# Hybrid decoder block: the output projection as seven block products, with the block sums made on GpSimd and the second token half finished tile by tile

## The chip, the cores and the metric

The kernel runs on one core of one Trainium2 chip. The metric is device time per execution in microseconds. The kernel before takes 1583.07 us, the median of three runs (1582.68 to 1584.89).

## The reference

One decoder block on 1024 tokens of width 1024, in float32. The step that changes is the one between the two branches and the FFN:

```python
merged = jax.nn.sigmoid(gate_a) * branch_a + jax.nn.sigmoid(gate_b) * branch_b
x = x + merged @ w_out[l]

h2 = rms_norm(x, ln2_g[l])
x = x + (jax.nn.silu(h2 @ w_ffn_gate[l]) * (h2 @ w_ffn_up[l])) @ w_ffn_down[l]
```

`branch_a` is the retention branch times `w_ret_out`, `branch_b` the attention branch times `w_attn_out`. `w_out` is 1024 x 1024.

## The kernel before, in words

Every float32 matrix product is made of three passes. Each operand is split into a high half (a rounded copy, type float32r, made by ScalarE) and a low half (the operand less the high half, made by VectorE); the passes are high x high, high x low and low x high, added up in PSUM. A helper `halves` or `split` is one such pair of instructions.

Most of the large products (the value projection, the gates, the FFN) already run in a form with seven block products in place of eight (the Strassen-Winograd form): each operand is cut into 2 x 2 blocks, sums of blocks are made first, and seven products P1 to P7 are added up in PSUM in such an order that each output block comes from one or two banks. The output projection does not; it runs as a plain product.

The order of the stages around the change:

- Branch A (`ba{n}`, lines 1103 to 1114). For each of 8 row blocks n of 128 features, `dense` loads a 512 KB slab of `w_ret_out`, splits it and makes 48 matmuls, 24 for each half of 512 tokens. `evac` then reads the gate `ta` and the other branch's part `mb` from DRAM, makes the merged row block `ms` on VectorE (two instructions) and splits it into the tiles M[0] and M[1] (tag B of the pool `act`). These hold the merged matrix transposed: features on the partitions, tokens along the row.
- Output projection (lines 1247 to 1304). x is loaded into x2. For each half `nh` of 512 output columns, the four slabs of `w_out` are loaded and split ahead; then for each of the 8 token tiles t, 24 matmuls (8 feature blocks x 3 passes) fill one PSUM bank of the tag `acc` (three banks in turn), and VectorE adds half of it to x2 (line 1283; the factor of a half belongs to the gates).
- In the second half of columns a token tile is complete, and its work up to the FFN's operands follows: ScalarE squares the row with an accumulator (line 1288), GpSimd makes the reciprocal root (two small instructions, lines 97 and 99), ScalarE scales the row (line 1293), TensorE transposes it in eight 128 x 128 pieces, and VectorE multiplies by the norm's gain (`columns`, lines 1207 to 1234). For the first four tiles each 512 columns are also split into a high and a low half there; for the last four, VectorE makes three block sums. `s2_part` and `a22_part` split one token tile of two of those sums. `early_t` makes sums of FFN weights, `prep_to` splits FFN weights, `release` makes low halves that were held back.

What sets the order: each engine runs its instructions one after the other. A planner orders them by priority and by its own costs; `high_priority(offset=AHEAD)` moves the loads and splits of weights ahead. Inside `in_order(engines)` the instructions of these engines keep the order in which they are written. For VectorE and ScalarE such a block (`late`) begins at the last token tile, for TensorE (`first`) at the FFN's first product. All DMAs here are issued from SyncE (SP), one after the other; an issue that must wait holds those behind it. A tile of a pool that takes over the memory of earlier ones waits for all their readers; x2 takes the memory of the tiles of branch A's `evac`. In PSUM, an instruction that writes a bank waits for the one that still has to read it. There are eight banks: three of tag `acc`, one of `pv`, two of `s`, two of `t`.

The functions that the change touches:

## Time and profile before

| | us |
|---|---|
| median of the runs | 1583.07 |
| span of the profiled execution | 1583.3 |
| TensorE busy | 1570.7 (99%) |
| VectorE busy | 990.2 (63%) |
| ScalarE busy | 720.7 (46%) |
| GpSimd busy | 354.9 (22%) |

The profiled execution has a span of 1583.3 us from its first to its last instruction, 0.2 us from the median, so a sum made on the trace holds for the runs as it is. Branch A runs from 766 to 853 us of the span, the output projection from 853 to 946. In a row of the profile the engines are PE (TensorE's matmuls), PEld (its weight loads), DVE (VectorE), ACT (ScalarE), POOL (GpSimd) and SP (SyncE, the DMA issues); `wo<-wotw,m` says that a tile wo is written from the tiles wotw and m; L1283 is a line of the kernel. A time in square brackets is how long the engine sat idle before the instruction, and behind the arrow stands what ended the wait.

### The profile page before, as it was taken

The numbers are of one execution on the slowest core, as the hardware profiler recorded it, in microseconds if no ns is written. First come the engines' busy times: TensorE is split into PE (matmuls) and PEld (weight loads), VectorE is DVE, ScalarE is ACT, GpSimd is POOL, SyncE is SP. The second block draws the span as 40 slices with busy tenths as digits, with TensorE's granted clock in tenths as the row PEclk, the third lists the DMA queues.
The fourth block names the chain that finished last, engine by engine and source line by source line (L and its number), as shares of the span: only waits on it lengthen the run. The fifth ranks groups of instructions, "written<-read, shape, count | busy, mean of one in ns | idle before, by whom it ended". The sixth has DMA issues, their size and how long they took to land.

```text
span 1583.3 us, 20873 instructions
## 1 busy us (share of the span) xinstructions
PE 1570.7 (99%) x7483; PEld 1307.1 (83%) x7483; DVE 990.2 (63%) x1776; ACT 720.7 (46%) x1446; POOL 354.9 (22%) x303
## 2 busy tenths in 40 slices
PE   9999999999999999999999999999999999999998
PEld 8887888888888888888888888888888888888886
DVE  6469978777657663878544369444444444678656
ACT  5258877844233333544221256333333333344445
POOL 2000000000055441000000013555555555100001
PEclk9999999999999999999999999999999999999999
DMA  6564655440364455654545102333333333762333
GB/s 204 157 176 124 205 193 150 143 140 34 126 225 150 134 166 184 229 189 156 177 149 199 54 0 74 106 104 106 112 105 100 101 110 109 285 250 84 98 103 124
DMA packets 148886, 223.13 MB, mean 141 GB/s; under 512 B 9195, under 2 KB 81709, under 8 KB 147246
## 3 DMA queue, kind: packets, MB, share of 16 engines
q1 hardware_dynamic: 148780, 221.79, 43.3%
q8 instruction: 59, 0.97, 0.3%
q14 instruction: 45, 0.37, 0.1%
q10 hardware_dynamic: 2, 0.00, 0.0%
HBM read 149.67 MB, written 67.37 MB: 137 GB/s over the span
## 4 chain that ended last, share of the span: by engine, by line
PE 90%; ACT 6%; DVE 3%; issue 1%; POOL 0%; POOLq 0%; ACTq 0%; DVEq 0%
PE fA L1337 15%; PE fB L1337 8%; PE dA L1618 7%; PE wA L841 7%; PE dxP L1618 6%; PE fC L1337 4%; PE wB L841 3%; PE va L686 3%; ACT sc L466 2%; PE acc_g L157 2%; PE vP L686 2%; PE acc_g L158 2%; PE acc_g L159 2%; PE wo L1277 2%; PE wo L1276 2%; PE acc_ba L159 2%
## 5 line engine op out<-in xcount | busy, mean ns | idle before, releaser
L1618 PE MATMUL dA<-dwP,daP 128*128 128x512 f32 x528 | 120.6, 389 | 0.0
L1618 PEld LDWEIGHTS dA<-dwP,daP 128*128 128x128 f32 x528 | 99.0, 188 | 20.7 <-DVE dwP L133 0.2
L1618 PE MATMUL dxP<-dwP,daP 128*128 128x512 f32 x396 | 90.2, 389 | 0.0
L1618 PEld LDWEIGHTS dxP<-dwP,daP 128*128 128x128 f32 x396 | 74.3, 188 | 15.4
L157 PE MATMUL acc_g<-h,wh_g 128*128 128x512 f32 x192 | 75.5, 393 | 0.1
L158 PE MATMUL acc_g<-h,wh_g 128*128 128x512 f32 x192 | 75.2, 392 | 0.0
L159 PE MATMUL acc_g<-h,wl_g 128*128 128x512 f32 x192 | 75.1, 393 | 0.0
L466 ACT ACTIVATE sc<-sc,nm 128x257 f32<-128x257 f32 (+1 forms) x128 | 62.5, 492 | 27.1 <-DVE nm L463 26.7
L451 POOL COPY sc<-nsink 128x4 f32<-128x4 f32 x32 | 13.1, 412 | 274.4 <-PE pT L484 157.1
L1406 POOL TENSOR_TENSOR xf<-xf 128x512 f32<-128x512 f32 x40 | 61.2, 1531 | 30.4 <-issue 28.9
L1348 POOL TENSOR_TENSOR xf<-xf 128x512 f32<-128x512 f32 x33 | 49.4, 1496 | 54.3 <-ACT t_1P L130 22.4
L463 DVE CUSTOM_DVE_ANT_0 sc<-s,amask,nsink 128x256 f32<-128x256 f32 (+1 forms) x128 | 54.1, 461 | 9.8 <-PE s L460 9.5
L1358 ACT COPY xf<-fA 128x512 f32<-128x512 f32 x44 | 25.7, 586 | 74.4 <-PE fA L1337 74.4
L133 DVE TENSOR_TENSOR dwP<-wd,dwP 128x512 fp32r<-128x512 f32 x77 | 52.8, 685 | 6.0 <-ACT dwP L130 6.0
L130 ACT CAST dwP<-wd 128x512 fp32r<-128x512 f32 x77 | 47.4, 616 | 9.4 <-PE dA L1618 7.1
L157 PE MATMUL acc_bb<-ay,wh_bb 128*128 128x512 f32 x128 | 51.2, 400 | 0.0
L1523 POOL TENSOR_TENSOR rs_f<-tot,mhalf 128x1 f32<-128x1 f32 x8 | 4.8, 606 | 205.4 <-DVE tot L1520 205.4
L158 PE MATMUL acc_bb<-ay,wh_bb 128*128 128x512 f32 x128 | 50.3, 393 | 0.0
L159 PE MATMUL aq<-h,wl_aq 128*128 128x512 f32 x128 | 50.2, 392 | 0.0
L157 PE MATMUL aq<-h,wh_aq 128*128 128x512 f32 x128 | 50.1, 392 | 0.0
L158 PE MATMUL aq<-h,wh_aq 128*128 128x512 f32 x128 | 50.1, 391 | 0.0
L159 PE MATMUL acc_bb<-ay,wl_bb 128*128 128x512 f32 x128 | 50.1, 391 | 0.0
(794 smaller groups left out, 4356.9 us busy)
## 6 DMA issues: line engine op xcount, KB each, us to landing
act_d<-xf SPq DMA_DIRECT2D x77, 256.0 KB, 2.1
daP<-act_d SPq DMA_DIRECT2D x21, 512.0 KB
q_d<-stg SPq DMA_DIRECT2D x8, 1024.0 KB
q<-q_d SPq DMA_DIRECT2D x32, 256.0 KB, 6.5
ay_d<-q SPq DMA_DIRECT2D x8, 1024.0 KB
ay<-ay_d SPq DMA_DIRECT2D x4, 2048.0 KB, 14.2
wr_daP<-act_d SPq DMA_DIRECT2D x14, 512.0 KB, 3.7
wr_g<-in_w_in SPq DMA_DIRECT2D x12, 512.0 KB, 5.9
```

The lines of the kernel that those rows point to most:

```text
L133: return nc.vector.tensor_tensor(out=lo, in0=raw, in1=f32(hi), op=ALU.subtract)
L157: nc.tensor.matmul(pt, hi[:, k, :], xh, start=(k == 0), stop=False)
L158: nc.tensor.matmul(pt, hi[:, k, :], xl, start=False, stop=False)
L159: nc.tensor.matmul(pt, lo[:, k, :], xh, start=False, stop=(k == 7))
L463: nc.vector.tensor_tensor_reduce(out=sc[:, j, 0:nk], in0=pt[:, jj * 256:jj * 256 + nk], in1=mk, scale=1.0, scalar=nsink[:, 4 * g + j:4 * g ...
L466: nc.scalar.activation(sc[:, j, 0:nk + 1], sc[:, j, 0:nk + 1], AF.Exp, scale=-1.0, bias=nm[:, j:j + 1], accum_out=den[:, j:j + 1])
L686: nc.tensor.matmul(vbanks[pr][tt], x_[:, c], w[:, u, :], start=(fresh and k + z == 0), stop=(k == 3 and z == 2), skip_group_check=not fresh)
L841: nc.tensor.matmul(pt, o[:, w, k, :], v, start=(first and k + z == 0), stop=(k == 3 and z == 2), skip_group_check=not first)
L1337: nc.tensor.matmul(pt, o[:, w, k, :], v, start=(first and k + z == 0), stop=(k == 3 and z == 2), skip_group_check=not first)
L1348: nc.gpsimd.tensor_tensor(out=dst[q], in0=dst[q], in1=sg[q], op=ALU.mult)
L1406: nc.gpsimd.tensor_tensor(out=o, in0=a, in1=b, op=op)
L1618: nc.tensor.matmul(banks[tt], a[:, u, c], w[:, v, :], start=(fresh and f + z == 0), stop=(f == NP - 1 and z == 2), skip_group_check=not fresh)
```

## The change

The output projection becomes seven block products. The merged matrix is cut into four blocks by feature half (kh) and token half, `w_out` into b11, b12, b21, b22. P1, P2 and P4 take blocks of the merged matrix as they are. P3, P5, P6 and P7 take sums of blocks.

Branch A runs its row blocks in the order 0, 4, 1, 5, 2, 6, 3, 7, so that after each second one the four blocks' rows are there; GpSimd makes four sums of 128 x 512, and each is stored to a DRAM tensor `ms_d`. Only three of the four blocks are split in `evac`. In the projection the sums are loaded back (1 MB each, `load_sum`) into the place of the low half and split there (`sum_halves`). The sums of `w_out` are made on VectorE and GpSimd (`sub2`), the halves of the weights in `wsplit`, two steps of 1024 columns each.

P2, P1, P5 and P6 run whole (`by_k`, 48 matmuls each). Then P3 runs by token tile for the first token half (`by_t`, 12 matmuls for each tile), and P7 and P4 by token tile for the second. P1, P6, P7 and P4 use the same four banks `vbank` one after the other; P2, then P5 and P3, use the banks of the tags `s` and `t`. `gain` adds a bank to one half of the columns of x2. `ln2_a` is the square and the reciprocal root, `ln2_b` the scaling. The blocks `late` and `first` now begin before P2. The block sums of the token tiles 4 and 5 in `columns` move from VectorE to GpSimd. The places of the FFN's operands in M[0] and M[1] (m0, m1) change with the products.

```diff
--- before.py
+++ after.py
@@ -63,6 +63,7 @@
     v_d = dram.tile([P, NB, D], F32, name="v_d")
     rk_d = dram.tile([8, P, S], F32, name="rk_d")
     rg_d = dram.tile([8, P, S], F32, name="rg_d")
+    ms_d = dram.tile([4, 4, P, 512], F32, name="ms_d")
     act_d = dram.tile([7, NF // 2, P, 512], F32, name="act_d")
 
     def ps(tag, bufs, name):
@@ -1090,28 +1091,41 @@
 
 
     M = [None, None]
-
-    def mview(k, t, z):
-        return M[k // 4][:, t, (2 * (k % 4) + z) * P:(2 * (k % 4) + z) * P + P]
-
     wdp = ctx.enter_context(tc.tile_pool(name="wdp", bufs=2, side="right"))
     with tc.tile_pool(name="w3", bufs=1) as w3:
-        for n in range(8):
-            if n % 4 == 0:
-                big(M, "B", n // 4, f"m{n // 4}")
+        for n in range(2):
+            big(M, "B", n, f"m{n}")
+        m0, m1 = (m.rearrange("p (q a) (b c) -> p q (a b) c", q=4, b=2) for m in M)
+        places = {(0, 0): (m0, 0), (1, 0): (m0, 2), (1, 1): (m1, 2)}
+        parts = {}
+        for n in (0, 4, 1, 5, 2, 6, 3, 7):
+            kh, k = n // 4, n % 4
 
             def evac(half, pt):
                 c = slice(half * 512, half * 512 + 512)
                 mb = w3.tile([P, 512], F32, tag="mb", bufs=3, name="mbr")
                 nc.sync.dma_start(mb, mb_d[n, :, c])
-                s = w3.tile([P, 512], F32, tag="ms", bufs=2, name="ms")
                 ta = w3.tile([P, 512], F32, tag="ta", bufs=3, name="tar")
                 nc.sync.dma_start(ta, tb_d[n, :, c])
+                s = w3.tile([P, 512], F32, tag=f"ms{kh}{half}", bufs=2, name=f"ms{kh}{half}")
                 nc.vector.scalar_tensor_tensor(out=s, in0=ta, scalar=1.0, in1=pt, op0=ALU.add, op1=ALU.mult)
                 nc.vector.tensor_tensor(out=s, in0=s, in1=mb, op=ALU.add)
-                s = s.rearrange("p (t s) -> p t s", s=P)
-                halves(s, *(mview(n, slice(4 * half, 4 * half + 4), z) for z in range(2)))
+                if (kh, half) in places:
+                    v, q = places[kh, half]
+                    halves(s, v[:, q, k, :], v[:, q + 1, k, :])
+                parts[kh, half] = s
             dense(w_ret_out, n * P, YG, evac, f"ba{n}")
+            if kh:
+                a11, a21, a12, a22 = (parts.pop(i) for i in ((0, 0), (0, 1), (1, 0), (1, 1)))
+                nc.gpsimd.tensor_tensor(out=a22, in0=a21, in1=a22, op=ALU.add)
+                nc.sync.dma_start(ms_d[0, k], a22)
+                nc.gpsimd.tensor_tensor(out=a21, in0=a11, in1=a21, op=ALU.subtract)
+                nc.sync.dma_start(ms_d[2, k], a21)
+                nc.gpsimd.tensor_tensor(out=a11, in0=a22, in1=a11, op=ALU.subtract)
+                nc.sync.dma_start(ms_d[1, k], a11)
+                nc.gpsimd.tensor_tensor(out=a12, in0=a12, in1=a11, op=ALU.subtract)
+                nc.sync.dma_start(ms_d[3, k], a12)
+
 
 
     w4 = ctx.enter_context(tc.tile_pool(name="w4", bufs=1))
@@ -1227,7 +1241,7 @@
                 nc.vector.tensor_tensor(out=a1[:, 2 * q + 1, :, c], in0=o, in1=f32(hi), op=ALU.subtract)
         if half:
 
-            eng = nc.vector
+            eng = nc.gpsimd if t < 6 else nc.vector
             a11, a12, a21, a22 = (xf[:, q, :, c] for q in range(4))
             eng.tensor_tensor(out=a21, in0=a21, in1=a22, op=ALU.add)
             eng.tensor_tensor(out=a11, in0=a21, in1=a11, op=ALU.subtract)
@@ -1235,80 +1249,203 @@
 
     def s2_part(t):
         c = slice(t % 4 * P, t % 4 * P + P)
-        halves(xf[:, 0, :, c], s12[:, 0, :, c], s12[:, 1, :, c])
+        halves(xf[:, 0, :, c], m0[:, 0, :, c], m0[:, 1, :, c])
 
     def a22_part(t):
         c = slice(t % 4 * P, t % 4 * P + P)
-        halves(xf[:, 3, :, c], s3a[:, 0, :, c], s3a[:, 1, :, c])
-
-
-    s12, s3a = (m.rearrange("p (q a) (b c) -> p q (a b) c", q=4, b=2) for m in M)
-
-    for t in range(NB):
-        nc.sync.dma_start(x2[:, t, :], x[t * P:t * P + P, :])
-    for nh in range(2):
-        nsl = slice(nh * 512, nh * 512 + 512)
...
-        else:
-            a1 = act.tile([P, 4, 4, 512], F32R, tag="A", name="a1")
-            xf = act.tile([P, 4, 4, 512], F32, tag="A", name="xf")
-            load(0)
-            load(1)
-        for t in range(NB):
-            pt = acc(f"wo{nh}{t}")
-            for k in range(8):
-                hi, lo = ws[k // 2]
-                mh, ml = mview(k, t, 0), mview(k, t, 1)
-                nc.tensor.matmul(pt, mh, hi[:, k % 2, :], start=(k == 0), stop=False)
-                nc.tensor.matmul(pt, mh, lo[:, k % 2, :], start=False, stop=False)
-                nc.tensor.matmul(pt, ml, hi[:, k % 2, :], start=False, stop=(k == 7))
-            if nh == 1 and t == NB - 1:
-                late = in_order(nc.vector.engine, nc.scalar.engine)
-                late.__enter__()
-                prep_to(2)
-                prep_to(4, True)
-            nc.vector.scalar_tensor_tensor(out=x2[:, t, nsl], in0=pt, scalar=0.5, in1=x2[:, t, nsl], op0=ALU.mult,
-                                           op1=ALU.add)
-            if nh == 1:
...
+        halves(xf[:, 3, :, c], m1[:, 0, :, c], m1[:, 1, :, c])
+
+
+    def blk(y, z):
+        return w_out[y * 512:y * 512 + 512, z * 512:z * 512 + 512].rearrange("(k p) n -> p k n", p=P)
+
+    def two(v, c):
+        return v[:, 2 * c:2 * c + 2]
+
+    def slots4(tags, name):
+        return [[slot(t_, [2, 512], F32R, f"wo{name}{c}{u}") for u, t_ in enumerate(tags)] for c in range(2)]
+
+    def wsplit(src, dst, eng=None):
+        for c in range(2):
+            nc.scalar.copy(dst[c][0], src[c])
+            (eng or nc.vector).tensor_tensor(out=dst[c][1], in0=src[c], in1=f32(dst[c][0]), op=ALU.subtract)
+
+    def sub2(eng, o, p, q):
+        for c in range(2):
+            eng.tensor_tensor(out=o[c], in0=p[c], in1=q[c], op=ALU.subtract)
+
+    W = {}
+    with tc.high_priority(offset=AHEAD):
+        b11, b21 = raw_pair([2, 512], "b11"), raw_pair([2, 512], "b21")
+        for y, b in ((1, b21), (0, b11)):
+            for c in range(2):
+                nc.sync.dma_start(b[c], two(blk(y, 0), c))
+        W["P2"] = slots4(("tw", "tw"), "P2")
+        wsplit(b21, W["P2"])
+        wdp.tile([P, 56], F32, name="pad_wdp", bufs=1)
+        W["P1"] = slots4(("wh", "wl"), "P1")
+        wsplit(b11, W["P1"])
+
+    wob = act.tile([P, 16, 512], F32, tag="A", name="wob")
+    sA = act.tile([P, 4, 4, 512], F32R, tag="A", name="sA")
+    b12, b22, t2 = ([two(wob[:, 4 * i:4 * i + 4], c) for c in range(2)] for i in range(3))
+    XA = {"P1": (m0, 0), "P2": (m0, 2), "P3": (m0, 0), "P4": (m1, 2), "P5": (sA, 0), "P6": (sA, 2), "P7": (m1, 0)}
+
+    def load_sum(pr, i):
+        v, q = XA[pr]
+        nc.sync.dma_start(f32(v[:, q + 1]), ms_d[i].rearrange("k p t -> p k t"))
+
+    def load_x(half, z):
+        nc.sync.dma_start(x2[:, 4 * half:4 * half + 4, z * 512:z * 512 + 512],
+                          x[half * 512:half * 512 + 512, z * 512:z * 512 + 512].rearrange("(t p) n -> p t n", p=P))
+
+    def sum_halves(pr):
+        v, q = XA[pr]
+        for c in range(2):
+            hi, lo = two(v[:, q], c), two(v[:, q + 1], c)
+            nc.scalar.copy(hi, f32(lo))
+            nc.vector.tensor_tensor(out=lo, in0=f32(lo), in1=f32(hi), op=ALU.subtract)
+
+    wide = [[m0[:, 2 + u, 2 * c:2 * c + 2, :] for u in range(2)] for c in range(2)]
+
+    nc.sync.dma_start(wob[:, 0:4], blk(0, 1))
+    load_sum("P5", 0)
+    load_x(0, 0)
+    nc.sync.dma_start(wob[:, 4:8], blk(1, 1))
+    load_sum("P6", 1)
+    load_sum("P7", 2)
+    load_x(1, 1)
+    load_x(0, 1)
+    load_x(1, 0)
+
+    vbank = [ps("pv", 1, "wo0"), acc("wo1"), acc("wo2"), acc("wo3")]
+    obank = {}
+
+    def obanks(pr):
+        obank[pr] = [ps("s", 2, f"wo{pr}{i}") for i in range(2)] + [ps("t", 2, f"wo{pr}{i}") for i in (2, 3)]
+        return obank[pr]
+
+    def wmm(pr, k, tt, first, last, tracked):
+        v, q = XA[pr]
+        bank = (obank["P5" if pr == "P3" else pr] if pr in ("P2", "P5", "P3") else vbank)[tt]
+        w = W[pr][k // 2]
+        c = slice(tt * P, tt * P + P)
+        for z, (u, y) in enumerate(((0, 0), (0, 1), (1, 0))):
+            nc.tensor.matmul(bank, v[:, q + u, k, c], w[y][:, k % 2, :], start=(first and z == 0), stop=(last and z == 2),
+                             skip_group_check=not tracked)
+
+    def by_k(pr, hooks=()):
+        fresh = pr in ("P2", "P1", "P5")
+        for k in range(4):
+            for tt in range(4):
+                wmm(pr, k, tt, fresh and k == 0, k == 3, fresh)
+            if k in dict(hooks):
+                dict(hooks)[k]()
+
+    def by_t(pr, tt):
+        for k in range(4):
+            wmm(pr, k, tt, False, k == 3, False)
+
+    def gain(half, tt, z, bank):
+        v = x2[:, 4 * half + tt, z * 512:z * 512 + 512]
+        nc.vector.scalar_tensor_tensor(out=v, in0=bank, scalar=0.5, in1=v, op0=ALU.mult, op1=ALU.add)
+
+    lnr = {}
+
+    def ln2_a(t):
+        m2 = tiny.tile([P, 1], F32, tag="m2", name="m2")
+        hxs[t] = wo.tile([P, D], F32, tag="hx", bufs=2, name="hx")
+        nc.scalar.activation(hxs[t], x2[:, t, :], AF.Square, scale=1.0 / 32.0, accum_out=m2)
+        lnr[t] = rstd_of(m2, 1, f"ln2_{t}")
+
+    def ln2_b(t):
+        nc.scalar.activation(hxs[t], x2[:, t, :], AF.Copy, scale=lnr[t])
+
+    late = in_order(nc.vector.engine, nc.scalar.engine)
+    late.__enter__()
+    first = in_order(nc.tensor.engine)
+    first.__enter__()
+
+    obanks("P2")
+    sub2(nc.vector, b11, b12, b11)
+    sum_halves("P5")
+    sum_halves("P7")
+    by_k("P2")
+
+    for tt in range(4):
+        gain(0, tt, 0, obank["P2"][tt])
+    W["P5"] = slots4(("tw", "tw"), "P5")
+    wsplit(b11, W["P5"])
+    sub2(nc.gpsimd, t2, b22, b11)
+    load(0)
+    sub2(nc.gpsimd, b21, b21, t2)
+    sub2(nc.gpsimd, b12, b22, b12)
+    by_k("P1")
+
+    for tt in range(4):
+        gain(0, tt, 0, vbank[tt])
+    load_sum("P3", 3)
+    W["P6"] = wide
+    wsplit(t2, W["P6"])
+    sum_halves("P6")
+    obanks("P5")
+    by_k("P5")
+
+    for tt in range(4):
+        gain(1, tt, 1, obank["P5"][tt])
+    W["P3"] = slots4(("wh", "wl"), "P3")
+    wsplit(b22, W["P3"])
+    sum_halves("P3")
+    W["P7"] = slots4(("tw", "tw"), "P7")
+    wsplit(b12, W["P7"])
+    by_k("P6")
+
+    W["P4"] = wide
+    wsplit(b21, W["P4"], nc.gpsimd)
+    load(1)
+    a1 = act.tile([P, 4, 4, 512], F32R, tag="A", name="a1")
+    xf = act.tile([P, 4, 4, 512], F32, tag="A", name="xf")
+    for tt in range(4):
+        gain(0, tt, 1, vbank[tt])
+    for tt in range(4):
+        by_t("P3", tt)
+        gain(0, tt, 1, obank["P5"][tt])
+        ln2_a(tt)
+        if tt > 1:
+            columns(tt - 2)
+        ln2_b(tt)
+    early_t(0, 2)
+    for tt in range(4):
+        t = 4 + tt
+        by_t("P7", tt)
+        gain(1, tt, 1, vbank[tt])
+        if tt == 0:
+            columns(2)
+        by_t("P4", tt)
+        if tt == 3:
+            prep_to(2)
+            prep_to(4, True)
+        gain(1, tt, 0, vbank[tt])
+        ln2_a(t)
+        if tt == 3:
+            release()
+        columns(t - 1)
+        ln2_b(t)
+        if tt == 0:
+            early_t(1, 2)
+        if tt > 1:
+            s2_part(t - 2)
+        if 0 < tt < 3:
+            a22_part(t - 1)
+    s2_part(6)
+    prep_to(5)
 
     s4 = [slot("tw", [2, 512], F32R, f"s4{z}") for z in range(4)]
     prep_to(6)
 
     X = {}
-    for pr, (t_, q) in {"P1": (a1, 0), "P2": (a1, 2), "P6": (s12, 0), "P5": (s12, 2), "P7": (s3a, 2),
-                        "P4": (s3a, 0)}.items():
+    for pr, (t_, q) in {"P1": (a1, 0), "P2": (a1, 2), "P6": (m0, 0), "P5": (m1, 2), "P7": (m0, 2),
+                        "P4": (m1, 0)}.items():
         X[pr] = [(t_[:, q, k, :], t_[:, q + 1, k, :]) for k in range(4)]
     X["P3"] = [(s4[k // 2][:, k % 2, :], s4[2 + k // 2][:, k % 2, :]) for k in range(4)]
 
@@ -1436,8 +1573,6 @@
     LA = 4
     f1 = None
     early = []
-    first = in_order(nc.tensor.engine)
-    first.__enter__()
     for i, (j, pr) in enumerate(seq):
         if i == 16:
             first.__exit__(None, None, None)
@@ -1460,13 +1595,13 @@
                 for z in range(2):
                     k = slice(2 * z, 2 * z + 2)
                     halves(src[:, k], hi[:, k], lo[:, k])
-            pieces(xf[:, 2], s12[:, 2], s12[:, 3])
+            pieces(xf[:, 2], m1[:, 2], m1[:, 3])
             prep_to(8)
 
             for z in range(2):
                 k = slice(2 * z, 2 * z + 2)
                 nc.vector.tensor_tensor(out=xf[:, 0, k], in0=xf[:, 3, k], in1=xf[:, 0, k], op=ALU.subtract)
-            pieces(xf[:, 0], s3a[:, 2], s3a[:, 3])
+            pieces(xf[:, 0], m0[:, 2], m0[:, 3])
             prep_to(10)
             early_t(0, 4)
             a22_part(NB - 2)
```

33 lines of the change are left out of this document (removed).

## The prediction

> **What bounds the kernel now.** I read the page first, for the engine that sets the time.
>
> ```profile
> span 1583.3 us, 20873 instructions
> ...
> PE 1570.7 (99%) x7483; PEld 1307.1 (83%) x7483; DVE 990.2 (63%) x1776; ACT 720.7 (46%) x1446; POOL 354.9 (22%) x303
> ...
> PEclk9999999999999999999999999999999999999999
> ...
> PE 90%; ACT 6%; DVE 3%; issue 1%; POOL 0%; POOLq 0%; ACTq 0%; DVEq 0%
> ```
>
> TensorE (PE) is busy 99% of the span at full granted clock and carries 90% of the chain of waits. A matmul removed is time gained, as long as PE is never made to wait; a wait put on PE is time lost one for one. Next the busy time by stretches: branch A (766 to 853 us), the first and second column half of the output projection (853 to 897, 903 to 946).
>
> ```profile
> 766.00:853.00 87.00, 87.00 (x387) 72.06 (x386) 44.41 (x59) 20.27 (x27) 0.00 (x0) 1.00 0.55 173
> 853.00:897.00 44.00, 44.00 (x196) 36.44 (x195) 10.84 (x14) 4.91 (x6) 0.00 (x0) 1.00 0.30 110
> 897.00:903.00 6.00, 6.00 (x28) 4.99 (x27) 3.96 (x6) 0.99 (x1) 0.00 (x0) 1.00 0.94 316
> 903.00:946.00 43.00, 43.00 (x218) 36.08 (x217) 25.76 (x40) 23.57 (x36) 7.88 (x14) 1.00 0.01 3
> ```
>
> The columns are the stretch's length, busy us (and instructions) of PE, weight load, DVE, ACT and POOL, then clock, DMA share and GB/s. PE is busy for the whole of every row: no wait is left in this stage. POOL (GpSimd) does nothing until 897. The instructions of the two stages, first and last start:
>
> ```profile
> L157 PE MATMUL acc_ba<-yg,wh_ba x128: 389/389/478, 766.1 to 852.5; 128*128 128x512 f32 x128
> ...
> L1275 PE MATMUL wo<-wotw,m x64: 389/389/477, 853.2 to 943.6; 128*128 128x512 f32 x64
> ...
> L1277 PE MATMUL wo<-wowh,m x64: 389/389/393, 855.0 to 945.4; 128*128 128x512 f32 x64
> ```
>
> A matmul lasts 389 ns, but they are pipelined: branch A's 384 take 87.0 us, 0.2267 us each. That pitch, not 389 ns, is what one is worth. The chain of waits around the end of the stage:
>
> ```profile
> 945.79 0.87 PE h2T L1215 x8
> 946.66 5.46 PE fA L1337 x24
> 952.12 0.87 PE h2T L1215 x8
> 953.00 5.46 PE fC L1337 x24
> ```
>
> Eight transposes of one token tile cost PE 0.87 us, and the last tile's VectorE work is covered by 24 matmuls of the FFN, 5.46 us. The change keeps both.
>
> **The change part by part.** *Matmuls.* Before: 2 column halves x 8 tiles x 24 = 384. After: 7 products x 48 = 336. 48 fewer x 0.2267 = **-10.9 us**. The eight sets of transposes stay.
>
> *Sums in branch A.* 16 POOL additions and 16 stores of 256 KB. The nearest rows:
>
> ```profile
> L1406 POOL TENSOR_TENSOR xf<-xf 128x512 f32<-128x512 f32 x40 | 61.2, 1531 | 30.4 <-issue 28.9
> ...
> act_d<-xf SPq DMA_DIRECT2D x77, 256.0 KB, 2.1
> ```
>
> 4 x 1.53 = 6.1 us on POOL in every 21.8 us (two row blocks), on an engine that is idle there; DVE and ACT lose the splitting of one quarter of the blocks. Cost: nothing, hidden behind branch A's matmuls at 55% DMA share. Only the last four are exposed. On SP's queue there are 14 issues more (16 stores, 4 loads of sums, 4 fewer of x, 2 fewer of w_out), half a microsecond each by the row below, in a queue that has less than one issue per us to make.
>
> ```profile
> 856.59 4.20 SPq L1248 DMA_DIRECT2D x<-in_x  x8
> ```
>
> *Loads of the first products.* The last block sum of branch A is known at 854.8. What follows it now:
>
> ```profile
> 854.13 0.69 DVE L1111 TENSOR_TENSOR ms<-ms,mbr 128x512 f32<-128x512 f32 x1
> ...
> 861.80 0.69 DVE L1283 SCALAR_TENSOR_TENSOR x<-wo,x 128x512 f32<-128x512 f32 x1 [5.24 <-DMA x<-in_x]
> ```
>
> ```profile
> GB/s 0 0 0 0 0 0 0 0 0 0 0 82 174 282 206 364 419 406 406 419 419 419 419 419 419 419 419 419 419 419 387 210 0 0 0 0 0 0 0 0
> ```
>
> (slices of 0.63 us from 850 to 875 us). Four POOL additions end at 856.4, 857.9, 859.4, 861; each store lands 2.1 us later. Then P5's sum (1 MB) is issued at 858.6, P7's at 860, P6's at 861.6, and the first quarter of x at 863, since x2 takes the memory that the last sums leave. At some 0.41 MB per us, 2.5 us per MB, and about 2 us before the first bytes, they land at 863, 865.6, 868 and 870.6. DVE and ACT are in written order here: split P5's sum, split P7's sum, four gains of P2 (which need that x), then split P5's weights. The prices of a split of 1024 and of ordinary 512 steps:
>
> ```profile
> 843.86 1.22 DVE L133 TENSOR_TENSOR wowl<-wrx_wo,wowh 128x1024 fp32r<-128x1024 f32 x1
> ...
> 895.34 1.06 ACT L130 CAST wotw<-wr_wo 128x1024 fp32r<-128x1024 f32 x1
> ...
> 901.44 0.69 DVE L1183 TENSOR_TENSOR wr_f<-wrx_f,wr_f 128x512 f32<-128x512 f32 x1 [2.00 <-DMA wrx_f<-in_w_ffn_gate]
> ...
> 938.58 0.69 DVE L559 TENSOR_TENSOR m<-xf,m 128x512 fp32r<-128x512 f32 x1 [0.83 <-ACT m L558]
> ```
>
> Gains 870.6 to 873.2, first half of P5's weights 874.4. PE reaches P5 after P2 and P1, at 853.1 + 2 x 10.9 = 874.9. I take **0**, but the cover is half a microsecond. If SP instead issues in written order, with the load of b12 behind the four stores (861) and 6.3 MB ahead of P7's sum, that sum lands at 878.5, and P5 starts near 885.8: **+10.9**. These are the ends; I stay at the lower, since b12 and b22 are ready from 850.5. The other weight work (POOL's t2, b21, b12, the splits of P6, P3, P7) ends 5 us or more before its product.
>
> *Second half, tile by tile.* This decides. One token tile's work in the kernel now, DVE, ACT and POOL of the same tile:
>
> ```profile
> 907.81 0.69 DVE L1283 SCALAR_TENSOR_TENSOR x<-wo,x 128x512 f32<-128x512 f32 x1 [1.98 <-PE wo L1277]
> 908.42 1.28 DVE L1223 TENSOR_TENSOR xf<-h2T,bcol 128x512 f32<-128x512 f32 x2
> 910.23 0.69 DVE L1227 TENSOR_TENSOR a<-xf,a 128x512 fp32r<-128x512 f32 x1 [0.53 <-ACT a L1226]
> 912.39 0.69 DVE L1227 TENSOR_TENSOR a<-xf,a 128x512 fp32r<-128x512 f32 x1 [1.46 <-ACT a L1226]
> ```
>
> ```profile
> 908.54 1.06 ACT L1288 ACTIVATE hx<-x 128x1024 f32<-128x1024 f32 x1 [1.09 <-DVE x L1283]
> 909.51 0.18 ACT L1288 ACTIVATION_READ_ACCUMULATOR hx<-x 128x1 f32 x1
> 909.60 0.60 ACT L1226 CAST a<-xf 128x512 fp32r<-128x512 f32 x1
> 910.69 1.15 ACT L1293 ACTIVATE hx<-x,rs_ln 128x1024 f32<-128x1024 f32 x1 [0.49 <-POOL rs_ln L99]
> ```
>
> ```profile
> 909.78 0.22 POOL L97 TENSOR_SCALAR ve_ln<-m 128x1 f32<-128x1 f32 x1 [3.51 <-ACT hx L1288]
> 910.08 0.58 POOL L99 TENSOR_TENSOR rs_ln<-ve_ln,mhalf 128x1 f32<-128x1 f32 x1
> ```
>
> From gain to last low half DVE needs 5.3 us (907.8 to 913.1), with waits for ACT inside. Today PE brings a tile every 6.3 us (5.44 + 0.87) and nothing on PE waits for a gain: the next tile goes to another bank. After the change P7 and P4 of a tile follow each other on the same bank, and DVE must read P7's result between them (gain on column half 1), else P4 would be added to it. So PE waits for that gain, and the gain stands in DVE's written order behind everything of the tile before: its last gain, two multiplies and low halves, t-sums, the P3-sum splits, each behind ACT. I follow them with 0.65 us per DVE step (1.28 for two), 0.60 per ACT cast, 1.24 for the square with its accumulator, 0.95 for POOL's two, 1.12 for the scaling, and 0.25 from DVE's end to the next matmul. Time 0 is the end of the tile's P4 on PE, which would be ready for the next P4 at 0.87 + 12 x 0.2267 = 3.6.
>
> - P4 of tile 6: gain 0.7, square 2.0, POOL 3.0, scaling 4.1, ACT half of the a22 piece 4.7, DVE half 5.4, gain 6.05, P4 at 6.3: wait 2.7.
> - P4 of tile 7: one more split pair ahead of it (s2 piece of tile 4): 3.4.
> - P4 of tile 5: gain 0.7, square 2.0, cast, low, multiply, cast, low 5.3, two weight sums 6.6, gain 7.3, P4 at 7.5: 3.9, and DVE comes 0.9 late from the tile before: 4.8.
> - P4 of tile 4: from tile 0's transposes (907.1) DVE has 12 steps, 7.8 us, and waits 6.2 for ACT, where tile 1's scaling, tile 2's square and tile 3's square stand between the casts; with 0.25 P4 starts 14.2 later. PE brings P3 of tile 3, tile 1's transposes, P7 and tile 2's transposes, 7.2 us: 7.0 (1.2 of it ahead of tile 2's transposes).
> - Tile 0's transposes: its reciprocal root stands on POOL behind the split of P4's weights (two of 1024, 2 x 3.06 from 897.8): 1.4.
>
> Sum **+19.3 us**. The lower end of the waits: DVE free whenever P7 ends, then each P4 waits for the gain alone, 0.69 + 0.25, in four tiles 3.8 us.
>
> The longest wait of PE for another engine in this trace is short, so nothing here shows PE after a longer one:
>
> ```profile
> PE warm L266 <- DVE wk L240: 1.0, 1, 1.0
> ```
>
> The Trainium skill, page "TensorE: Matmul & The Clock Gate", Part 1, says that PE's clock falls to half after an idle window of about 3.4 us and comes back after a busy one; by that two or three of my waits would be followed by a slow patch, and no run here shows it.
>
> *Sum.* -10.9 + 0 + 0 + 19.3 = +8.4 us on the profiled execution: 1583.3 + 8.4 = 1591.7. That execution's span lies 0.2 us above the median, 1583.07, so I forecast **1591.5 us**.
>
> **The rivals.**
>
> (a) *DVE keeps up.* If the tile chain fits under 3.6 us of PE, each P4 waits only for its own gain: -10.9 + 3.8 = -7.1, **1576**. For it: POOL takes the three sums of tiles 4 and 5. Against: the 5.3 us chain above, and the written order on DVE and ACT. It turns faster once all waits together are under 10.9 us.
>
> (b) *Waits near the saving.* Without the backlog at tiles 4 and 5 (7.0 and 4.8 become 3.0 and 3.9), waits of 13 less a few steps of DVE at 0.60: **1580 to 1586**, no change.
>
> (c) *P5's operands late*, by SP's order or by transfers that share the queues, up to +10.9: **1602**. For it: margin 0.5 us. Against: 419 GB/s in the row above, all 16 engines.
>
> (d) *A slow clock after the two longest waits*: 12 matmuls each at twice 0.2267, +2.7 twice: **1597**. For it: nothing in this trace, whose clock is 1.00 in every row; against it: nothing either. It is the page's rule above.
>
> (e) *P7 waits as well.* The a22 pieces write the block that P7 reads, other columns of it. If the planner takes this as a conflict, P7 of tiles 6 and 7 starts behind the piece (5.5 instead of 0.9) and P4 one gain later: 2.9 more in each, **1597**.
>
> **How the numbers follow.** Forecast 0.45, with 1588 to 1595 as its own range; (a) 0.11, (b) 0.12, (c) 0.15, (d) 0.12, (e) 0.05. A measurement of this kernel tells some 0.2%, 3.2 us, from no change. Faster (below 1580): (a) and the edge of (b), 0.13; same 0.12; slower 0.75. The range goes from (a) to (c): 1577 to 1602.
>
> **What would show it.** In the profile after: 336 matmuls of the projection; PE waits for DVE on the bank of the P7 and P4 products, four of them, 2.7 to 6 us; DVE's idle time before the low halves put down to ACT. P5's first matmul within 1 us of P1's last, or (c). A granted clock below 1 after the long waits, or (d). The saving alone, with PE busy in every row between 853 and 936, would prove me wrong; so would waits at P4 near 1 us.

## The result, and the profile after

The changed kernel takes **1607.04 us** (median of 4 runs, 1604.04 to 1609.28) against 1583.98 us (1582.68 to 1584.96, 4 runs) for the kernel before on the same chip: ratio 1.0147, 95% interval 1.0133 to 1.0162. It is 23 us slower, where I had forecast 8.4, and it lies above the end of my range.

The page after, span and engines:

```profile
span 1602.2 us, 20889 instructions
PE 1563.7 (98%) x7435; PEld 1298.7 (81%) x7435; DVE 1020.0 (64%) x1792; ACT 730.7 (46%) x1456; POOL 406.4 (25%) x333
```

48 matmuls are gone (7483 before, 7435 now) and PE's busy time fell by 7.0 us, yet the span grew by 18.9: PE now waits. The view of PE's waits (engine, line and tile; what it waited for; us in total, times, longest):

```profile
PE wo L1334 <- DVE x L1351: 13.9, 4, 4.7
PE woP L1334 <- DVE x L1351: 7.7, 1, 7.7
PE woP L1334 <- DVE woP L1271: 2.1, 1, 2.1
PE h2T L1229 <- DVE xf L1237: 1.9, 2, 1.2
```

None of these rows exists before, where the longest wait of PE for another engine was 1.0. L1351 is `gain`: four waits of P4's matmuls, and one of P5's. PE's timeline through the stage (start, us, instruction; in square brackets the idle time before it):

```profile
880.31 0.76 PE L1334 MATMUL woP<-woP,sA 128*128 128x512 f32 x1 [7.66 <-DVE x L1351]
883.14 12.36 PE L1334 MATMUL woP<-woP,sA 128*128 128x512 f32 x47 [2.07 <-DVE woP L1271]
895.34 11.04 PE L1334 MATMUL wo<-m,sA 128*128 128x512 f32 x48
906.22 8.33 PE L1334 MATMUL woP<-woP,m 128*128 128x512 f32 x36
...
927.66 4.36 PE L1334 MATMUL wo<-m,m 128*128 128x512 f32 x12 [2.65 <-DVE x L1351]
...
939.13 3.02 PE L1334 MATMUL wo<-m,m 128*128 128x512 f32 x12 [3.46 <-DVE x L1351]
...
948.81 3.02 PE L1334 MATMUL wo<-m,m 128*128 128x512 f32 x12 [3.06 <-DVE x L1351]
...
952.46 2.98 PE L1334 MATMUL wo<-woP,m 128*128 128x512 f32 x12
960.17 5.10 PE L1334 MATMUL wo<-m,m 128*128 128x512 f32 x12 [4.73 <-DVE x L1351]
...
965.90 3.00 PE L1474 MATMUL fA<-a,t_0P 128*128 128x512 f32 x12
```

The stage begins with P2 at 850.73 and the FFN's first product starts at 965.90: 115.2 us. Before, PE's timeline has it from 853.21 to 946.42, 93.2 us. So the stage is 22.0 longer, which is -10.9 for the matmuls and **+32.9** of losses. (In this execution branch A begins 2.5 us earlier than before, ahead of any edited line; that is no gain of the change, and the runs of before differ among themselves by 2.3. Where times of the two are compared below, they are counted from the start of P2.) The losses fall into two places:

- **P5**, 12.0 us. P1 ends at 872.49; P5 would take 10.88, and P6 starts at 895.34.
- **The tile loops**, 21.0 us. From 906.22 to 965.90 are 59.7 us, for 144 matmuls (32.6) and seven sets of transposes (6.1).

In both, some of the loss is no wait: 12 matmuls of P4 last 4.36 and 5.10 where others last 3.02, and P5's 47 last 12.36 where 10.8 are due (P6's 48 last 11.04). The rows by stretches show it in the granted clock (the third number from the end), then DMA share and GB/s:

```profile
865.00:877.00 12.00, 7.65 (x34) 6.01 (x32) 6.66 (x3) 3.26 (x4) 12.00 (x5) 0.96 1.03 381
877.00:890.00 13.00, 7.62 (x25) 5.87 (x26) 13.00 (x16) 8.31 (x9) 0.35 (x1) 0.65 0.84 295
...
915.00:930.00 15.00, 10.47 (x50) 8.17 (x49) 9.65 (x16) 8.32 (x12) 1.76 (x5) 0.90 0.01 1
...
960.00:975.00 15.00, 14.83 (x64) 12.28 (x65) 10.25 (x17) 7.58 (x17) 0.79 (x2) 0.84 0.00 0
766.00:850.70 84.70, 84.70 (x375) 70.16 (x374) 42.28 (x52) 16.68 (x21) 16.77 (x12) 1.00 0.59 196
```

The last row is branch A: PE is busy all 84.7 us while GpSimd makes 12 sums. That part is hidden, as predicted.

**Why P5 is late.** The timelines of SP's issues, then of DVE, ACT and POOL between branch A and P5:

```profile
861.36 0.32 SPq L1127 DMA_DIRECT2D ms_d<-ms  x1
861.78 0.37 SPq L1296 DMA_DIRECT2D sA<-ms_d  x1
863.64 0.38 SPq L1299 DMA_DIRECT2D x<-in_x  x1
...
864.62 0.53 SPq L1296 DMA_DIRECT2D m<-ms_d  x1
```

```profile
868.65 6.49 DVE L1307 TENSOR_TENSOR sA<-sA 128x1024 fp32r<-128x1024 f32 x2 [11.20 <-ACT sA L1306]
876.82 2.74 DVE L1307 TENSOR_TENSOR m<-m 128x1024 fp32r<-128x1024 f32 x2 [1.69 <-ACT m L1306]
879.49 2.47 DVE L1351 SCALAR_TENSOR_TENSOR x<-woP,x 128x512 f32<-128x512 f32 x4
881.88 1.21 DVE L1271 TENSOR_TENSOR woP<-wr_b,woP 128x1024 fp32r<-128x1024 f32 x1
```

```profile
867.56 2.01 ACT L1306 CAST sA<-sA 128x1024 fp32r<-128x1024 f32 x2 [14.57 <-DMA sA<-ms_d]
875.75 1.99 ACT L1306 CAST m<-m 128x1024 fp32r<-128x1024 f32 x2 [6.18 <-DMA m<-ms_d]
```

```profile
854.16 2.21 POOL L1120 TENSOR_TENSOR ms<-ms,ms 128x512 f32<-128x512 f32 x1 [15.12 <-DVE m L560]
...
868.34 2.41 POOL L1275 TENSOR_TENSOR wrx_b<-wrx_b,wob 128x1024 f32<-128x1024 f32 x1
870.70 6.65 POOL L1275 TENSOR_TENSOR wob<-wob 128x1024 f32<-128x1024 f32 x2
```

P5's sum needs only the first store, but SP issues its load behind all four, at 861.78; it lands at 867.5. P7's sum, last of the loads named here and on queues that are full, lands at 875.7. ACT and DVE stand in written order, in which the split of **P7's** sum comes before P2's gains and before the low halves of P5's weights. So P5's first matmul waits for a gain that waits for an operand of a product three places later. Besides, the low halves of P5's sum take DVE 6.49 us for two, where the same step takes 2.35 elsewhere, while POOL's two differences beside them take 6.65. And the block sums themselves come late: POOL's first one waits for DVE's split of the last block, and it and the second take 2.21 and 2.15 where the third and fourth take 1.29.

In the tile loops the same pair of engines shows. The change moved the block sums of tiles 4 and 5 to POOL, and the two splits that DVE makes beside those of tile 5, just ahead of the gain for which tile 7 waits 4.73, take 2.67 us for two, where the prediction's row has 0.69 for one; POOL's sums run from 954.67 to 958.97:

```profile
956.85 2.67 DVE L560 TENSOR_TENSOR m<-xf,m 128x512 fp32r<-128x512 f32 x2 [3.09 <-ACT m L559]
```

### The profile page after: what moved, and what is told of

Same layout as the page of the kernel before. It is cut to its first block, busy times and chain, and to the rows that moved or that the text cites. A ratio compares the mean times of both kernels' runs of the same rounds, so it can differ in the third digit from the quotient of the medians.

```text
span 1602.2 us, 20889 instructions
## 1 busy us (share of the span) xinstructions
PE 1563.7 (98%) x7435; PEld 1298.7 (81%) x7435; DVE 1020.0 (64%) x1792; ACT 730.7 (46%) x1456; POOL 406.4 (25%) x333
## 4 chain that ended last, share of the span: by engine, by line
PE 83%; ACT 6%; DVE 4%; issue 2%; DMA 2%; POOL 1%; SPq 0%; POOLq 0%; DVEq 0%; ACTq 0%
PE fA L1474 15%; PE fB L1474 7%; PE dA L1753 7%; PE wA L842 6%; PE dxP L1753 6%; PE fC L1474 4%; PE wB L842 3%; PE va L687 3%; PE acc_g L158 2%; PE acc_g L159 2%; PE acc_g L160 2%; PE vP L687 2%; ACT sc L467 2%; PE acc_bb L158 2%; PE acc_bb L159 2%
## 5 line engine op out<-in xcount | busy, mean ns | idle before, releaser
L556 POOL TENSOR_TENSOR wr_wp<-wr_wp 128x512 f32<-128x512 f32 x10 | 16.6, 1657 | 140.0 <-DVE w0P L134 122.5
L131 ACT CAST daP<-daP 128x512 fp32r<-128x512 f32 x42 | 26.0, 620 | 54.1 <-PE dxP L1753 26.7
L158 PE MATMUL aq<-h,wh_aq 128*128 128x512 f32 x128 | 50.2, 392 | 0.0
```

What stands on the lines that cost most here:

```text
L131: nc.scalar.copy(hi, raw)
L158: nc.tensor.matmul(pt, hi[:, k, :], xh, start=(k == 0), stop=False)
```

## The experiments

My theory after this reading: all the losses come from the order in which DVE's and ACT's work is written, plus one contention (DVE with POOL) and one consequence (a slow clock after PE's waits). The rivals were that P5 waits for transfers as such, that the shared bank of P7 and P4 forces the loop's waits by itself, and that the long matmuls have some other cause than the waits.

**P7's split behind the splits it does not have to precede.**

```diff
     sum_halves("P5")
-    sum_halves("P7")
     by_k("P2")
...
     wsplit(b12, W["P7"])
+    sum_halves("P7")
     by_k("P6")
```

> One line is moved: the split of P7's sum (two steps on ACT and DVE) stands behind the split of P7's weights instead of ahead of P2's gains. Theory A: the wait of TensorE ahead of P5 (P1 ends at 872.5, P5 runs from 883.1 in the changed kernel) is the load of P7's sum, fourth in the queue, on which DVE and ACT wait in written order. Then P5 starts when P5's sum, the first quarter of x and P5's weights are done: 868.65 + 6.5 (the two low halves as measured) + 2.5 + 1.2 = 879, 4 us sooner, and less of it at a slow clock: 1601 to 1603 against 1607. Theory B: the round trip of P5's own sum through DRAM is the bound, not P7's: P5 starts where it did, 1607.

Measured: 1605.84 us (1604.07 to 1607.98), ratio to before 1.0137 (1.0122 to 1.0152). PE's timeline and DVE's row for P5's low halves:

```profile
878.22 0.47 PE L1334 MATMUL woP<-woP,sA 128*128 128x512 f32 x1 [3.24 <-DVE x L1351]
881.05 13.54 PE L1334 MATMUL woP<-woP,sA 128*128 128x512 f32 x47 [2.36 <-DVE woP L1271]
```

```profile
870.91 6.56 DVE L1307 TENSOR_TENSOR sA<-sA 128x1024 fp32r<-128x1024 f32 x2 [11.13 <-ACT sA L1306]
```

The wait fell from 7.66 to 3.24, 4.4 us as expected, so the written order did hold P5. But the matmuls behind it run longer here (13.54), and in this execution, the slowest of the four, P4's four groups last 4.61, 5.49, 4.59 and 4.99, 4.2 us more together than after the change, whose profile is of its fastest run. So the wait is shown, but the time of the whole kernel (1604.07 to 1607.98 beside 1604.04 to 1609.28) does not show a gain clear of the scatter; I had given the waits a price and the clock behind them none.

**The same, with two differences of the weights on DVE, behind P5's gains, in place of POOL beside P5's split.**

```diff
-    sub2(nc.gpsimd, b21, b21, t2)
-    sub2(nc.gpsimd, b12, b22, b12)
     by_k("P1")
...
         gain(1, tt, 1, obank["P5"][tt])
+    sub2(nc.vector, b12, b22, b12)
+    sub2(nc.vector, b21, b21, t2)
```

> e1_p7_split_late, and the two weight differences b21 and b12 (four steps of 1024) on DVE behind P5's gains instead of on POOL right away. In e1 the two low halves of P5's sum took 6.56 us on DVE while POOL made those differences, against 2.35 for two elsewhere. Theory D: DVE and POOL slow each other when both read two operands from SBUF. Then the low halves take 2.35 us, and P5 starts when the first quarter of x is in, four gains and one split later, 877 instead of 881 on e1's time axis: 1606 - 4 - 1 = 1601. Otherwise the 6.56 us stay (a wait for the sum's second half, say) and so does the time.

Measured: 1602.85 us (1601.46 to 1603.34), ratio 1.012 (1.0105 to 1.0135).

```profile
870.98 2.36 DVE L1307 TENSOR_TENSOR sA<-sA 128x1024 fp32r<-128x1024 f32 x2 [11.19 <-ACT sA L1306]
```

```profile
874.83 0.39 PE L1334 MATMUL woP<-woP,sA 128*128 128x512 f32 x1
876.92 10.99 PE L1334 MATMUL woP<-woP,sA 128*128 128x512 f32 x47 [1.70 <-DVE woP L1271]
...
909.10 1.09 PE L1229 MATMUL h2T<-ident,hx 128*128 128x128 f32 x8 [2.15 <-ACT hx L1362]
```

With POOL quiet the low halves take 2.36, not 6.56, starting at the same time: the contention is shown. P5 follows P1 at once; its loss falls from 12.0 to 2.0 us (874.83 to P6's start at 887.75, less 10.88), with no slow matmuls. No transfer was moved for this, so most of P5's wait was not for transfers as such. The gain is not kept whole: DVE has four steps of 1.22 more just ahead of the tiles, the first tile's reciprocal root now does wait behind POOL's split of P4's weights (2.15), and the transposes wait 1.8 us in place of 0.7.

**All of P7 ahead of all of P4**, so that a P4 tile waits only for a gain of four groups of matmuls ago. The rest of the loop's work stays with P4, and `columns(3)` goes behind P7's third tile.

```diff
     for tt in range(4):
-        t = 4 + tt
         by_t("P7", tt)
         gain(1, tt, 1, vbank[tt])
         if tt == 0:
             columns(2)
+        if tt == 2:
+            columns(3)
+    for tt in range(4):
+        t = 4 + tt
         by_t("P4", tt)
```

> All four tiles of P7 first, then all four of P4, with the same work behind each; nothing else. Theory A: P4 waits because the gain on the same bank stands in DVE's written order behind the tile before. With three other tiles between, the four waits (2.65, 3.46, 3.06 and 4.73 us idle) and the slow matmuls behind two of them (some 3.6 us) go; new waits of about 1.4 us at three transposes come in, since a tile's scaling takes 4 us and PE is there after 3.6: 1607 - 17.5 + 4 = about 1593. Theory B: DVE, ACT and POOL together need more than PE's 3.6 us for a tile wherever the gain stands: the waits move to the transposes and the time stays above 1602.

Measured: 1597.98 us (1596.16 to 1598.13), ratio 1.0084 (1.0069 to 1.0099). PE's waits:

```profile
PE h2T L1229 <- ACT hx L1362: 3.6, 2, 1.8
...
PE fA L1478 <- DVE t_0P L134: 1.7, 1, 1.7
```

The row of 13.9 us is gone, and the time lies between the two that I had expected. Of the 13.9, these two rows bring 5.3 back: the transposes now reach PE before the scaling of their rows is done, and the FFN's first product waits for its weights, because DVE and ACT have no less to do for each tile than before.

**The loop kept, the pieces written later.** P7 and P4 share a bank as in the change, but the splits of the second half's sums and the two weight sums (`early_t(1, 2)`) stand behind the next P7 gain and no longer ahead of it.

```diff
         gain(1, tt, 1, vbank[tt])
+        if tt == 1:
+            early_t(1, 2)
+        if tt > 1:
+            a22_part(t - 2)
+        if tt == 3:
+            s2_part(4)
...
-        if tt == 0:
-            early_t(1, 2)
-        if tt > 1:
-            s2_part(t - 2)
-        if 0 < tt < 3:
-            a22_part(t - 1)
+    s2_part(5)
```

> The tile loop of the changed kernel with P7 and P4 back to back as there; only the two weight sums and the a22 and s2 pieces are written behind the next tile's gain on P7 instead of ahead of it. Theory A1: the bank wait itself is short (a gain of 0.69 and some 0.25), and most of each wait is the written order on DVE ahead of that gain. Then the waits ahead of P4 of tiles 5, 6 and 7 fall from 3.46, 3.06 and 4.73 us to about 2.2, 0.9 and 0.9 (tile 5 keeps the low halves of tile 3 ahead of it), with less at a slow clock: 1607 - 7 - 2 = 1598. Theory A2: a wait for a bank costs 3 us or more by itself: 1607.

Measured: 1597.91 us (1596.0 to 1600.3), ratio 1.0091 (1.0076 to 1.0106). PE's timeline at the four P4 tiles:

```profile
927.78 5.49 PE L1334 MATMUL wo<-m,m 128*128 128x512 f32 x12 [2.65 <-DVE x L1351]
...
939.05 3.02 PE L1334 MATMUL wo<-m,m 128*128 128x512 f32 x12 [1.72 <-DVE x L1351]
...
946.48 3.04 PE L1334 MATMUL wo<-m,m 128*128 128x512 f32 x12 [0.78 <-DVE x L1351]
...
953.91 3.06 PE L1334 MATMUL wo<-m,m 128*128 128x512 f32 x12 [0.78 <-DVE x L1351]
```

The bank costs 0.78 us a tile, near my lower bound of 0.94 (a gain of 0.69 and its handing over); what was above it at tiles 6 and 7 (2.28 and 3.95) came from what stood ahead of the gain in DVE's written order, the splits slowed by POOL among it. A few moved lines are worth as much as the reordered products.

**The waits filled.** After the change, plus 24 transposes of the identity into a free bank ahead of each P4 tile: work without use, 2.78 us, about the shortest of the four waits (2.65).

```diff
             columns(2)
+        wpt = ps("t", 2, f"idle{tt}")
+        for _ in range(24):
+            nc.tensor.transpose(wpt[:, 0:P], ident, ident)
         by_t("P4", tt)
```

> The changed kernel with 24 transposes of the identity into a bank that is free, between P7 and P4 of each tile (2.6 us of TensorE, less than the waits there, results not used). Theory C: a slow clock follows an idle TensorE; with the waits filled, the 12 matmuls of P4 that took 4.36 and 5.10 us take 2.9 again, the granted clock from 915 to 975 is 1.00 and the time falls by about 3 us, to 1604. Without that mechanism the long matmuls come from something else and the time stays at 1607 or rises.

Measured: 1603.47 us (1601.68 to 1604.96), ratio 1.0123 (1.0106 to 1.014): 3.6 us **below** the changed kernel, with 96 instructions more on the bounding engine (the slowest run here and the fastest there overlap by 0.9). The rows by stretches:

```profile
915.00:930.00 15.00, 13.09 (x80) 10.92 (x79) 9.20 (x15) 8.40 (x13) 2.38 (x6) 1.00 0.00 1
...
960.00:975.00 15.00, 14.51 (x72) 12.17 (x73) 12.26 (x20) 9.15 (x20) 0.79 (x2) 1.00 0.00 1
```

The clock is 1.00 in both, and in the two rows between them, and P4's groups last 3.02 to 3.04. Unfilled, two of the four groups are long in the profile after, four with P7's split late and three with the differences on DVE. So the long matmuls come from the idle time ahead of them, and this is worth 3 to 4 us in the loops: 1.3 + 2.1 is what the two long groups of the profile after are above 3.0.

The Trainium skill, page "TensorE: Matmul & The Clock Gate", Part 1, says that the clock falls to half after an idle window of about 3.4 us and that this window runs free. The runs agree in kind: behind waits of about 3 us the same 12 matmuls last 3.02 in one run and 5.49 in another, while behind 4.73 they were long each time that the wait was not filled. In size they do not: matmuls behind 2.65 us, less than that window (with another wait of 1.2 just before it), lasted 4.36 to 5.49, and behind 3.46 us 3.02 in one run.

**Cures together.** Five kernels combine these edits.

The first takes the late split of P7 and the order P7, then P4.

> Both edits together. If the two waits have nothing to do with each other, the gains add: 1593 - 5 = 1588. If a later P5 only gave DVE time that the tile loop needs, less than the sum: 1590 to 1593.

Measured: 1591.5 us (1589.67 to 1594.36), ratio 1.0047 (1.0032 to 1.0062). Alone the two gave 1.2 and 9.1 us, together 15.5, so the waits do not simply take each other's place. (The time lies in the range that I had given to gains adding up to less than their sum; I had put each of the two alone too high.) With fewer waits less of the time seems to run at the slow clock (mean granted clock 0.994 to 0.997 in these runs, 0.988 to 0.993 after the change); that this makes the difference is not shown by a run of its own, and the 1.2 is not clear of the scatter.

The second adds the differences on DVE, puts the transposes two tiles behind P4, the splits of the FFN's weights ahead of the P4 tiles or between them, and the last transposes between the FFN's first two products:

```diff
+    early_t(1, 2)
+    prep_to(2)
     for tt in range(4):
         t = 4 + tt
         by_t("P4", tt)
         gain(1, tt, 0, vbank[tt])
         ln2_a(t)
-        if tt > 0:
-            columns(t - 1)
+        if tt > 1:
+            columns(t - 2)
         ln2_b(t)
+        if tt == 1:
+            prep_to(4)
```

> e6 and e2's order (all of P7, then all of P4), the transposes of a tile two tiles behind its P4 instead of one, the FFN's first weights split ahead of the P4 loop, and the transposes of tile 6 between the first two FFN products. From e3_both (1591.5): 4 to 5 less for P5 as in e6; the waits ahead of the transposes of tiles 4 and 6 (1.79 and 1.76) and in the first FFN product (0.46 and 1.96) go: 1591.5 - 4.5 - 5.5 = 1581, within 0.2% of the kernel before.

Measured: 1594.38 us (1593.39 to 1594.83), ratio 1.0067 (1.0052 to 1.0082), a miss of 13 us. DVE's timeline has the reason:

```profile
943.06 0.69 DVE L134 TENSOR_TENSOR t_0P<-wrx_f,t_0P 128x512 fp32r<-128x512 f32 x1 [6.46 <-ACT t_0P L131]
...
944.27 0.68 DVE L1351 SCALAR_TENSOR_TENSOR x<-wo,x 128x512 f32<-128x512 f32 x1
```

With `prep_to(4)` written behind tile 5, DVE stands 6.46 us on a cast that ACT makes only after its scaling, and the next gain stands behind it. It is the same fault as in the change, which I had built in anew.

The third is the second with the last block's later three stores issued from ACT's queue, so that SP can issue P5's load behind the first.

> e7, with the last three stores of the block sums (sums 2, 1 and 3 of the last row block) issued from ACT's queue. SP holds the load of P5's sum behind those three stores; now it is issued 2.1 us after the first store, some 3 us sooner. P5 then waits for the first quarter of x alone, which still needs the last store: 1 to 2 us less than e7, 1579.

Measured: 1595.81 us (1593.76 to 1597.4), ratio 1.008 (1.0063 to 1.0097), no gain, and 17 us above what I expected, which rested on the 1581 that the second had missed. P5's first matmul starts at 873.05 (P1 ends at 872.7), but the second still waits 2.36 for its weights' low halves. These stand behind P2's gains, and the gains were held by a load:

```profile
866.83 0.37 SPq L1300 DMA_DIRECT2D x<-in_x  x1
```

```profile
872.22 2.48 DVE L1352 SCALAR_TENSOR_TENSOR x<-woP,x 128x512 f32<-128x512 f32 x4 [3.07 <-PE wo L1335]
```

SP issues the first quarter of x 15.9 us behind P2's start (850.94), where it was 12.9 without this edit: it waits 7.6 us for a store of the sums. It lands 5.1 us after its issue, at 871.9, just ahead of the gains. (The view puts DVE's 3.07 us down to a matmul of P1, whose banks these gains do not read.) So P5's own load came sooner and x later, and nothing was won.

The fourth goes back to transposes one tile behind, with `prep_to(2)` between P7 and P4.

```diff
         if tt == 2:
             columns(3)
+    prep_to(2)
     for tt in range(4):
         t = 4 + tt
         by_t("P4", tt)
         if tt == 3:
-            prep_to(2)
             prep_to(4, True)
```

> All three cures at once, with the transposes one tile behind as in the changed kernel: P7's split late, two of the weight differences on DVE, all of P7 ahead of all of P4, and the first FFN weight splits ahead of the P4 tiles. Theory (PE's time is the sum of the waits that DVE's and ACT's written order makes, and nothing else is lost): before 1583.2 - 10.9 for the 48 matmuls, + 2.1 at P5, + 2.2 + 1.8 + 1.2 at the transposes of the first half (their root behind GpSimd's P4 split), + two waits of about 1.75 at the transposes of the second half, + 0.5: 1583 to 1585, no change. Rival (the matmuls saved are lost elsewhere as well): above 1588.

Measured: 1588.55 us (1586.88 to 1589.33, 8 runs) against 1583.28 (1582.72 to 1584.93, 11 runs), ratio 1.0027 (1.0017 to 1.0038): the best of the kernels here that have the change, and still slower than before. PE's timeline:

```profile
909.05 1.09 PE L1229 MATMUL h2T<-ident,hx 128*128 128x128 f32 x8 [2.15 <-ACT hx L1362]
...
938.32 1.75 PE L1229 MATMUL h2T<-ident,hx 128*128 128x128 f32 x8 [2.98 <-ACT hx L1362]
939.72 4.08 PE L1334 MATMUL wo<-m,m 128*128 128x512 f32 x12
```

The time lies where I had put the rival (above 1588), not the theory (1583 to 1585). The waits at P5 and in the first half have the sizes I had listed; one in the second half is larger (2.98 for 1.75), with a slow patch behind it. The FFN's first product on an operand of the second half starts 108.9 us behind P2 (853.08 to 961.93); before, it started 105.1 us behind the projection's start (853.21 to 958.29). Even with the cures that I found, the stage loses more than the 10.9 us that it saves.

The last makes the low halves of P4's weights on DVE, behind the first half's tiles.

> The same, with the low halves of P4's weights made on DVE behind the first token half's tiles and no longer on GpSimd ahead of them. Theory: the wait of 2.15 at the first tile's transposes (reciprocal root behind GpSimd's split) goes, GpSimd no longer slows DVE there, and the two splits of 1.22 on DVE lie beside P7's 10.9 us: 2 to 4 below the kernel it is made from, 1580 to 1583. Rival (DVE has no room left for 2.4 us): no gain, with a new wait at P7 or P4 in place of the old one.

Measured: 1591.61 us (1590.35 to 1594.3), ratio 1.0052 (1.0037 to 1.0067). PE's timeline:

```profile
927.30 0.63 PE L1229 MATMUL h2T<-ident,hx 128*128 128x128 f32 x4 [1.52 <-DVE xf L1237]
929.18 0.66 PE L1229 MATMUL h2T<-ident,hx 128*128 128x128 f32 x4 [1.26 <-DVE xf L1237]
```

The rival holds: DVE has no room for 2.4 us more here. Two new waits of 1.5 and 1.3 appear, and the old one at the first tile only falls from 2.15 to 1.74.

## Why the prediction was wrong, point by point

**The matmuls, right.** 48 fewer at 0.2267 us, PE busy for all of branch A, eight sets of transposes as before: the page after has 7435 matmuls for 7483, and -10.9 is what 48 are worth.

**The sums in branch A, right for twelve, wrong for the last four.** POOL's 12 sums in that stretch cost PE nothing. Its last four ended 10.6 us behind P2's start (861.33 less 850.73), where I had 7.9 (861 less 853.1): I started them at DVE's last sum, but the first waited for DVE's split of that block, and two of them ran at 2.2 us beside DVE where I had 1.53. The 861 in both is only the earlier start of that execution.

**P5's operands, the step that failed.** I wrote "I take **0**, but the cover is half a microsecond". It cost 12.0 us. Three terms of that step were wrong. First, counted from P2's start, SP issued P5's load at 11.1 us, behind all four stores, not at 5.5, and the sum landed at 16.8, not 9.9; P7's landed at 25.0, not 12.5, since four loads of 1 MB were issued within 2.8 us and three more right behind, at 381 GB/s. Second, I had named the split of P7's sum ahead of P2's gains as part of the chain and still left the chain with half a microsecond of room; the first experiment gives that order alone 4.4 us. Third, I priced DVE's split at 1.22 a step, from a row where POOL was idle, although my own list puts POOL's differences at the same time; the second experiment gives that 4.2 us on DVE. The two experiments together take the loss at P5 from 12.0 to 2.0 us. With such a margin, the upper end that I had worked out (10.9) was the better value.

**The tile loops, right in cause; the sum came near by luck.** I had 19.3; the loops lost 21.0, of which 15.8 are in the rows of waits for DVE (13.9 + 1.9), 3.4 are slow matmuls, and 1.8 lie in gaps without a name. The single terms were worse: tile 4 waits 2.65 (with 1.9 ahead of the two transposes before it) where I had 7.0, tile 5 3.46 for 4.8, tile 6 3.06 for 2.7, tile 7 4.73 for 3.4; the first tile's transposes do not wait at all as long as P5 is late, where I had 1.4. So terms that were too large and a slow clock that I had left out made up for each other. At tile 7 I had priced DVE's splits as if POOL were quiet, the mistake of P5 again: the pair took 2.67, not 1.3. That the waits come from DVE's written order was shown by the kernel with the pieces moved. The 0.25 us that I counted from DVE's end to the next matmul is in no row; the gain ahead of tile 5's P4 ends at 939.07 and PE starts at 939.13.

**The clock, the second step that failed.** I held "a slow clock after the two longest waits" as a rival with a chance of 0.12. But its condition was my forecast itself, which had waits of 7.0 and 4.8 in it: it belonged into the sum, not beside it. It measured 3.4 us in the loops and 1.6 at P5 (12.36 for 10.8) in the profiled execution. The other three runs are 2.8 to 5.2 us longer at mean clocks of 0.988 to 0.991 against 0.993.

**The rivals.** (a) and (b) fell: P4 waits 2.65 to 4.73, and even the cured kernels stay above 1586. (e) fell: P7's matmuls of tile 7 start at 952.46, right behind the eight transposes of 951.67. In (b), the 13 us leave out the 1.4 at the first tile's transposes. (c) and (d) came true, and not in place of the forecast but with it. With them the sum is 1583.07 - 10.9 + 19.3 + 10.9 + 5.4 = 1607.8, beside 1607.04 measured, but so close a fit is partly luck: (c) measured 12.0, without the load of b12 behind the stores from which I had worked it out (b12 was issued at 848.2, ahead of them); (d) measured 3.4 in the loops, not 5.4, and behind tiles 4 and 7, not 4 and 5; and the loops without the clock lost 17.6, not 19.3. My range reached to one of them at a time, so its upper end was 1602.

**What stays open.** That POOL's block sums make tile 7's wait 1.3 longer than I followed is read from the rows and was not tried by moving them back. The 1.8 us in gaps without a name were not looked into, nor why the same 12 matmuls are slow behind one wait of 3 us and not behind another.

## What to carry to other kernels

On a kernel whose bounding engine has no idle time, a saving of 11 us is lost as soon as each of a handful of steps waits 2 us for work that merely stands in the wrong place of another engine's written order; so follow the order, instruction by instruction, up to the first consumer, and move what is not needed yet behind it. Rivals that can happen together with the forecast belong into its sum and into the upper end of the range. A cover of half a microsecond under a chain of DMA, split and gain is no cover.

## What the runs showed of the hardware that was not expected

- DVE and POOL, both with two operands in SBUF, hold each other up. Two splits of 128x1024 take DVE 2.36 us with POOL quiet and 6.49 to 6.56 with POOL at such work, whose two differences then take 6.65 for 4.8. The Trainium skill, page "SBUF — State Buffer", section "SBUF: two separate sides", says that the pair of ports they share is held by one instruction at a time and that the other is blocked. The trace agrees: if each waits for the other's instruction in turn, DVE's first split waits from 868.65 for POOL's end at 870.75 and runs to 871.97, POOL's next runs to 874.3, and DVE's second ends at 875.5; it ended at 875.14.
- 2.8 us of idle transposes ahead of the matmuls that come after a wait make those 1.3 to 2.1 us shorter, so work without use paid for itself: 3.6 us between the medians, with ranges that overlap by 0.9.
- Gains can add up to more than their sum: 1.2 and 9.1 us alone, 15.5 together. The slow clock behind the waits is the likely cause, but no run here separates it.
